# A transformer block on one core: the first products taken on the input with the channel scale alone, the token's scale and the shifts applied behind the sums

## The chip, the cores and the metric

The kernel runs on one core of a Trainium2 chip. The metric is the time of one execution in microseconds (us) on the device; for a kernel several runs are made and their median is given. A profile is the hardware profiler's record of one further execution.

## The reference, cut to what matters

The block is a feed-forward layer, a token mixer and a second feed-forward layer on 512 tokens of 1024 channels, in float32. The change touches the very first step only:

```
mod = silu(c) @ w_ada + b_ada            # 9 x 1024 numbers; m[0] a shift, m[1] a scale
h = rmsnorm(x, ffn1_pre_g) * (1 + m[1]) + m[0]
y = (silu(h @ w_gate) * (h @ w_up)) @ w_down
```

With r(token) = 1 / sqrt(mean over channels of x*x + eps), gamma(channel) = g * (1 + m[1]) and beta(channel) = m[0], this is h = x * r * gamma + beta. Since r belongs to the token and gamma and beta to the channel that a product sums over, h @ w = r * ((x * gamma) @ w) + beta @ w.

## The kernel before, in words

**Tiling.** Everything is held transposed: channels lie on the 128 partitions, in 8 blocks k, and the 512 tokens along them. A product of float32 quality is made of three float32r products: operand and weights are each split into a rounded high part and the rest (`hi`, `lo`), and hi·hi, lo·hi and hi·lo are summed in a bank of PSUM. `split` (L213) does this for a block of weights: ScalarE copies it rounded (L217), VectorE subtracts (L221). Raw weights arrive in a ring of 3 buffers, the split ones lie in rings of 6. `self.w2` hands out work tiles of 128x512 from a pool of 6.

**The opening** is `start` (L526). Three pairs of gate and up tiles (NSTART = 3, so six banks) are summed over the 8 channel blocks in step with the arrival of the modulation weights `wa` (8 MB, groups of 1, 1, 2, 2 and 2 blocks) and of the weights `w0` (one 384 KB block for each k). For each group `mod_rows` (L592) multiplies silu(c) into `wa` on TensorE, ScalarE copies the rows out, `mod_cols` (L604) turns them into columns of gamma and beta, and makes the `hi` and `lo` of those blocks of h: two ScalarE instructions (L618, L619) and one of VectorE (L620) for a block, on `u` = x * r, which `prepare` (L622) has made (L627) together with the split of w0[k]. Before any of that the whole input is squared and summed (L635 to L641), TensorE adds over the partitions (L645), root and reciprocal follow, and four transposes spread the result over a tile (L651, L653): r. `busy(n)` issues products that nobody reads. `first_product` (L694) is one of the 144 products of the opening. Then `act_tile` (L697) makes silu(gate) * up for the three pairs, and the gate and up products of the other 19 pairs follow (`product`, L322 to L325), each 24 matmuls over the 8 blocks of h in order, each in the next free bank.

**What sets the order.** TensorE and the DMA queue of SyncE (SP) execute in the order in which the program is written. ScalarE, VectorE and GpSimd get an order from a planner, which goes by the program's order and by the times it reckons. The DMAs of the opening are all issued by SP: cols, the four quarters of x, ident, then `wa` and `w0` in turn; from the fourth w0 on each has to wait for a raw buffer. Two background tasks start in this stage: `mod_task` (L473), the rest of the modulation, and `presplit` (L258), which splits weights of later stages through four buffers that lie where x lies, and fetches x again when it is done (L280). It can begin when x is no longer read.

Of the kernel before, what the change touches and what calls it, by code (L numbers as in the profile page):

```python
# [5 lines left out]
F32 = mybir.dt.float32  # L6
# [3 lines left out]
AF = mybir.ActivationFunctionType  # L10
# [4 lines left out]
P = 128  # L15
S = 512
D = 1024
ND = D // P
# [92 lines left out]
class Build:  # L111
# [414 lines left out]
    def start(self):  # L526
        nc = self.nc
        c = self.const
        self.cols = c.tile([P, NCOLS], F32, name="cols")
        nc.sync.dma_start(self.cols, self.i["cols"])  # L530
        self.X = self.big("X", XS)
        self.xd = self.dram.tile([P, ND, S], F32, name="xd")
        for q in range(4):
            nc.sync.dma_start(self.X.tiles[q // 2][:, 2 * (q % 2):2 * (q % 2) + 2], self.i["x"][:, 2 * q:2 * q + 2])
        self.ident = c.tile([P, P], F32, name="ident")
        nc.sync.dma_start(self.ident, self.i["ident"])
        w0 = [None] * ND

        groups = ((0,), (1,), (2, 3), (4, 5), (6, 7))
        wa = {}  # L540

        def fetch(g):
            if g < 2:
                t = self.blk("wa", AS[g], shape=(P, 8, 256))
                wa[g] = [t[:, :4], t[:, 4:]]
                nc.sync.dma_start(t, self.i["wa0"][g])
            else:
                wa[g] = [self.blk("wa", (AS[2:], YS, WS)[g - 2][e], shape=(P, 4, 512)) for e in range(2)]
                for e in range(2):
                    nc.sync.dma_start(wa[g][e], self.i["wa2"][g - 2, e])  # L550

        def fetch_w(k):
            w0[k] = Load(self.i["w0"][k], (6, P))
            w0[k].raw = self.ring.tile([P, 6, P], F32, name="raw", tag="raw", bufs=RAW)
            nc.sync.dma_start(w0[k].raw, w0[k].src)
            self.waiting += 1
        fetch(0)
        fetch_w(0)
        fetch(1)
        fetch_w(1)  # L560
        fetch(2)
        fetch_w(2)

        self.ones = c.tile([P, P], F32, name="ones")
        nc.gpsimd.memset(self.ones, 1.0)
        self.eps = c.tile([P, 1], F32, name="eps")
        nc.vector.memset(self.eps, EPS)

        self.sel = c.tile([P, 1], F32, name="sel")
# [12 lines left out]
        for pt in rows:  # L582
            nc.vector.memset(pt, 0.0)
        idle = self.bank("mm")

        def busy(n):

            for _ in range(n):
                nc.tensor.matmul(idle[:, :P], self.ones, self.ones, start=True, stop=True)
        accs, us = {}, {}  # L590

        def mod_rows(g):  # L592


            n = 256 * len(groups[g])
            acc = accs[g] = self.small.tile([P, 512], F32, name="macc", tag="macc", bufs=2)[:, :n]
            pt = rows[g % 2]
            for k in range(8):
                q = k % 4
                nc.tensor.matmul(pt[32 * q:32 * q + 1, :n], self.cs[:, k:k + 1], wa[g][k // 4][:, k % 4],  # L600
                                 start=(k < 4), stop=(k >= 4))
            nc.scalar.activation(acc, pt[:, :n], AF.Copy)

        def mod_cols(g):  # L604

            pt = rows[g % 2]
            k0, n = groups[g][0], len(groups[g])
            for q in range(2 * n):
                nc.tensor.matmul(pt[:, q:q + 1], accs[g][:, q * P:(q + 1) * P], self.sel, start=True, stop=True)
            mk = self.modc[:, :16].rearrange("p (j d) -> p d j", d=8)[:, k0:k0 + n]  # L610
            bk = self.col("b_ada", 0, 16).rearrange("p (j d) -> p d j", d=8)[:, k0:k0 + n]
            nc.vector.tensor_tensor(mk, pt[:, :2 * n].rearrange("p (d j) -> p d j", j=2), bk, op=ALU.add)
            gm = self.modc[:, 8 + k0:8 + k0 + n]
            nc.vector.scalar_tensor_tensor(gm, gm, 1.0, self.col("g1pre", k0, n), op0=ALU.add, op1=ALU.mult)
            for k in groups[g]:
                gamma, beta = self.modc[:, 8 + k:9 + k], self.modc[:, k:k + 1]
                h32 = self.last_h = self.w2("h32")
                nc.scalar.activation(hi[k], us[k], AF.Identity, scale=gamma, bias=beta)  # L618
                nc.scalar.activation(h32, us[k], AF.Identity, scale=gamma, bias=beta)  # L619
                nc.vector.tensor_tensor(lo[k], h32, hi[k].bitcast(F32), op=ALU.subtract)  # L620

        def prepare(g):  # L622

            for k in groups[g]:
                self.split(w0[k])
                us[k] = self.w2("u")
                nc.vector.tensor_tensor(us[k], self.X[k], r, op=ALU.mult)  # L627

        with self.tc.manual_schedule(engines={mybir.EngineType.PE}):
            busy(34)  # L630

            totals = []
            for k in range(ND):
                sq = self.w2("sq")
                nc.scalar.activation(sq, self.X[k], AF.Square)  # L635
                if k < 2:
                    totals.append(sq)
                else:
                    nc.vector.tensor_tensor(totals[k % 2], totals[k % 2], sq, op=ALU.add)
            total = totals[0]  # L640
            nc.vector.tensor_tensor(total, total, totals[1], op=ALU.add)  # L641
            pt = self.bank("wo")
            s, s2 = [self.small.tile([P, 4], F32, name="s", tag="s4") for _ in range(2)]
            for q in range(4):
                nc.tensor.matmul(pt[:, q:q + 1], total[:, q * P:(q + 1) * P], self.ones[:, 0:1], start=True, stop=True)  # L645
            nc.scalar.activation(s, pt[:, :4], AF.Sqrt, bias=self.eps, scale=1.0 / D)
            nc.vector.reciprocal(s2, s)
            pb = self.bank("wo")
            mod_rows(0)
            for q in range(4):  # L650
                nc.tensor.transpose(pb[:, q * P:(q + 1) * P], s2[:, q:q + 1].to_broadcast([P, P]), self.ident)  # L651
            r = self.w2("r")
            nc.scalar.activation(r, pb, AF.Copy)  # L653
            prepare(0)
            mod_cols(0)
            mod_rows(1)
            busy(4)
            prepare(1)
            banks = [self.bank("mm") for _ in range(4)] + [self.bank("wo") for _ in range(2)]
            for gi, g in enumerate(groups):  # L660
                for k in g:
                    if k + 3 < ND:
                        fetch_w(k + 3)
                    if k < 2:
                        fetch(k + 3)
                    if k == ND - 1:

                        for j in range(2 * NSTART):
                            for part in range(3):
                                self.first_product(banks[j], w0[k], j, k, part)  # L670
                    for part in range(3 if k < ND - 1 else 0):
                        for j in range(2 * NSTART):
                            self.first_product(banks[j], w0[k], j, k, part)

                        if part == 0 and k == g[-1] and gi + 1 < len(groups):
                            mod_cols(gi + 1)
                    self.alive -= 1

                    if k == g[0]:
                        nx = gi + 2 if gi == 0 else gi + 1  # L680
                        if gi != 1 and nx < len(groups):
                            mod_rows(nx)
                            prepare(nx)
                    if k >= 6:
                        self.feed(k - 5)

        nc.scalar.activation(warm, self.last_h[:, 0:1], AF.Silu)
        for f in range(NSTART):
            self.act_tile(f, banks[2 * f], banks[2 * f + 1], FULL)

    def first_product(self, ps, l, j, k, part):
        hi, lo = self.h
# [746 lines left out]
```

## Time and profile before

| what | value |
|---|---|
| runs: median (lowest to highest) | 1057.77 us (1055.55 to 1059.27) |
| the profiled execution's own time | 1056.43 us |
| its span, first to last instruction | 1054.7 us |
| TensorE busy | 1038.6 us, 98% of the span |
| VectorE busy, ScalarE busy | 625.8 us (59%), 478.3 us (45%) |
| mean granted TensorE clock | 0.996 |

The span lies within the execution's time; 1.73 us are around it. TensorE is nearly always busy, so a time is read off its row of instructions: what it has to do, and when it stands still. A timeline gives the start, the busy length and, in brackets, the idle time ahead of an instruction and who ended it.

### The profile page before, as it was taken

Reading aid. Unit: us, or ns where it says so; the run is one execution under the profiler, and the core shown is the slowest. Engines: PE = TensorE matmul, PEld = TensorE weight load, DVE = VectorE, ACT = ScalarE, POOL = GpSimd, SP = SyncE. Lnnn points to the kernel's source line nnn. Section 1 sums busy time; section 2 is a strip of 40 time slices with the busy share of each in tenths; the row PEclk is TensorE's granted clock in tenths of the full one; section 3 lists DMA queues with packets and bytes.
Section 4 is the critical chain, followed back from the end, with each engine's and each line's share of the span. In section 5 each row is a group of like instructions: output and inputs, shape, how many; then the busy total and the mean of one; then the engine's idle time right before and its main releaser. Section 6 shows DMA issues by size and latency. Waiting matters only on the chain.

```text
span 1054.7 us, 15248 instructions
## 1 busy us (share of the span) xinstructions
PE 1038.6 (98%) x5884; PEld 882.5 (84%) x5884; DVE 625.8 (59%) x1167; ACT 478.3 (45%) x782; POOL 88.4 (8%) x155
## 2 busy tenths in 40 slices
PE   8999999999999999999999999999999999999996
PEld 7788888888888999987776579999888888888896
DVE  5587877887774246579997843776322334333345
ACT  6564444343333457456776544645232222222252
POOL 0111111111110000000302610000000000000000
PEclk9999999999999999999999999999999999999998
DMA  9899899989997569593544431444333223333312
GB/s 366 320 378 360 336 354 328 335 308 357 333 342 281 214 222 349 179 355 120 204 161 144 152 117 41 162 141 135 125 120 100 93 79 109 100 99 100 100 41 80
DMA packets 57912, 217.32 MB, mean 206 GB/s; under 512 B 7128, under 2 KB 9496, under 8 KB 53232
## 3 DMA queue, kind: packets, MB, share of 16 engines
q1 hardware_dynamic: 43072, 164.86, 43.8%
q0 software_dynamic: 14768, 51.49, 13.5%
q8 instruction: 46, 0.75, 0.3%
q14 instruction: 26, 0.21, 0.1%
HBM read 193.24 MB, written 25.19 MB: 207 GB/s over the span
## 4 chain that ended last, share of the span: by engine, by line
PE 94%; DMA 3%; ACT 1%; issue 1%; DVE 1%; SPq 0%; DVEq 0%; ACTq 0%
PE mm L323 14%; PE mm L324 14%; PE mm L325 14%; PE wo L323 9%; PE wo L324 9%; PE wo L325 9%; PE mm L317 3%; PE mm L318 2%; PE mm L320 2%; PE mm L1251 2%; PE mm L694 1%; PE wo L317 1%; PE aux L1292 1%; PE wo L318 1%; PE wo L320 1%; DMA raw<-in_win_dram 1%
## 5 line engine op out<-in xcount | busy, mean ns | idle before, releaser
L217 ACT ACTIVATE hi<-raw 128x1024 fp32r<-128x1024 f32 (+2 forms) x192 | 197.2, 1031 | 377.6 <-PE mm L324 163.4
L221 DVE TENSOR_TENSOR lo<-raw,hi 128x1024 fp32r<-128x1024 f32 (+2 forms) x145 | 170.3, 1178 | 137.7 <-ACT hi L217 136.7
L323 PE MATMUL mm<-hhi,hi 128*128 128x512 f32 x368 | 144.1, 392 | 0.0
L325 PE MATMUL mm<-hhi,lo 128*128 128x512 f32 x368 | 143.3, 389 | 0.0
L324 PE MATMUL mm<-hlo,hi 128*128 128x512 f32 x368 | 143.2, 389 | 0.0
L323 PE MATMUL wo<-hhi,hi 128*128 128x512 f32 x280 | 111.1, 397 | 0.0
L323 PE MATMUL mm<-ahi,hi 128*128 128x256 f32 (+1 forms) x330 | 109.8, 334 | 0.0
L324 PE MATMUL mm<-alo,hi 128*128 128x256 f32 (+1 forms) x330 | 109.7, 333 | 0.0
L325 PE MATMUL mm<-ahi,lo 128*128 128x256 f32 (+1 forms) x330 | 109.7, 333 | 0.0
L325 PE MATMUL wo<-hhi,lo 128*128 128x512 f32 x280 | 109.6, 391 | 0.0
L324 PE MATMUL wo<-hlo,hi 128*128 128x512 f32 x280 | 109.0, 389 | 0.0
L325 PEld LDWEIGHTS mm<-hhi,lo 128*128 128x128 f32 x368 | 69.1, 188 | 14.5
L324 PEld LDWEIGHTS mm<-hlo,hi 128*128 128x128 f32 x368 | 69.1, 188 | 14.1
L323 PEld LDWEIGHTS mm<-hhi,hi 128*128 128x128 f32 x368 | 69.1, 188 | 14.1
L471 DVE SCALAR_TENSOR_TENSOR macc<-wa,cs,macc 128x512 f32<-128x512 f32 x98 | 73.2, 747 | 1.5
L324 PEld LDWEIGHTS mm<-alo,hi 128*128 128x128 f32 x330 | 62.7, 190 | 6.0
L325 PEld LDWEIGHTS mm<-ahi,lo 128*128 128x128 f32 x330 | 62.6, 190 | 6.0
L323 PEld LDWEIGHTS mm<-ahi,hi 128*128 128x128 f32 x330 | 62.5, 190 | 6.0
L324 PEld LDWEIGHTS wo<-hlo,hi 128*128 128x128 f32 x280 | 52.6, 188 | 12.0 <-issue 1.2
L323 PEld LDWEIGHTS wo<-hhi,hi 128*128 128x128 f32 x280 | 52.6, 188 | 11.9 <-issue 1.0
L325 PEld LDWEIGHTS wo<-hhi,lo 128*128 128x128 f32 x280 | 52.6, 188 | 11.1 <-issue 0.2
L317 PE MATMUL mm<-hhi,hi 128*128 128x256 f32 x232 | 59.1, 288 | 1.4 <-ACT hhi L382 1.4
(272 smaller groups left out, 1967.2 us busy)
## 6 DMA issues: line engine op xcount, KB each, us to landing
raw<-in_gu_dram SPq DMA_DIRECT2D x89, 512.0 KB, 4.4
wa<-in_wa_dram SPq DMA_DIRECT2D x36, 1024.0 KB, 10.0
lo<-pre SPq DMA_DIRECT2D x47, 512.0 KB, 5.2
pre<-pre POOLq DMA_DIRECT2D x36, 512.0 KB, 7.1
raw<-in_dn_dram SPq DMA_DIRECT2D x32, 448.0 KB, 4.0
raw<-in_win_dram SPq DMA_DIRECT2D x26, 512.0 KB, 6.2
raw<-in_dn_dram SPq DMA_DIRECT2D x22, 512.0 KB, 4.0
pre<-in_win_dram POOLq DMA_DIRECT2D x21, 512.0 KB, 6.5
```

The source lines that it names most:

```text
L217: nc.scalar.activation(l.hi, l.raw, AF.Copy)
L221: nc.vector.tensor_tensor(l.lo, l.raw, l.hi.bitcast(F32), op=ALU.subtract)
L317: self.nc.tensor.matmul(ps, l.hi[:, kt], xh[kt][:, tok], start=(q == 0), stop=False)
L318: self.nc.tensor.matmul(ps, l.lo[:, kt], xh[kt][:, tok], start=False, stop=False)
L320: self.nc.tensor.matmul(ps, l.hi[:, kt], xl[kt][:, tok], start=False, stop=(q == n - 1))
L323: self.nc.tensor.matmul(ps, l.hi[:, kt], xh[kt][:, tok], start=(first and q == 0), stop=False)
L324: self.nc.tensor.matmul(ps, l.hi[:, kt], xl[kt][:, tok], start=False, stop=False)
L325: self.nc.tensor.matmul(ps, l.lo[:, kt], xh[kt][:, tok], start=False, stop=(last and q == n - 1))
L471: nc.vector.scalar_tensor_tensor(acc, w[:, k], ck, acc, op0=ALU.mult, op1=ALU.add)
L694: self.nc.tensor.matmul(ps, w[:, j], x[k], start=(k == 0 and part == 0), stop=(k == ND - 1 and part == 2))
L1251: nc.tensor.matmul(ps[:, :n], self.q[rows, g, i * P:(i + 1) * P], self.k[rows, g, :n], start=True, stop=False)
L1292: nc.tensor.matmul(ps[64 * e:64 * e + 64, :P], self.v[:, t, 64 * h:64 * h + 64], pts[e][:, t * P:(t + 1) * P], start=(t == 0), stop=(t == i))
```

## The change: what it does

The first products are made on x * gamma in place of h. r comes in when a sum is read from PSUM, and beta @ w as a column added there (`first_act`). In detail:

- The order of the DMAs is now cols, `wa` 0, x 0, `w0` 0, `wa` 1, `w0` 1, `wa` 2 (two halves), x 1, `w0` 2, ident; the third and fourth quarter of x follow inside the loop.
- `busy(34)` becomes `busy(18)`, and a `busy(2)` is added. `mod_rows(1)` and its `prepare` move behind the first six products of k = 0; for k = 0 and 1 the next `mod_cols` stands behind the second part of the three.
- In `mod_cols` a block's `hi` is one ScalarE copy of x with gamma as the scale, `lo` one VectorE instruction. A third, new one per block adds w0[k] * beta into a tile `shifts`. The squares of x and their sums are made here, group by group.
- `scales` runs in three steps: the sum over partitions of two tiles (8 matmuls of one column, behind k = 4), the transposes, r and the load of the Silu table (inside k = 5), and the sum of `shifts` over the partitions (6 matmuls of one column, inside k = 7).
- The remaining 19 pairs still need the true h. `whole(k, r)` makes it in the same place: u = x * r, hi and the full value on ScalarE, lo on VectorE; blocks 0 to 5 behind k = 5, block 6 behind k = 6, block 7 behind the second `first_act`.

```diff
         fetch(0)
+        fetch_x(0)
         fetch_w(0)
         fetch(1)
         fetch_w(1)
         fetch(2)
+        fetch_x(1)
         fetch_w(2)
+        nc.sync.dma_start(self.ident, self.i["ident"])
...
             for k in groups[g]:
-                gamma, beta = self.modc[:, 8 + k:9 + k], self.modc[:, k:k + 1]
-                h32 = self.last_h = self.w2("h32")
-                nc.scalar.activation(hi[k], us[k], AF.Identity, scale=gamma, bias=beta)
-                nc.scalar.activation(h32, us[k], AF.Identity, scale=gamma, bias=beta)
-                nc.vector.tensor_tensor(lo[k], h32, hi[k].bitcast(F32), op=ALU.subtract)
+                gamma = self.modc[:, 8 + k:9 + k]
+                nc.scalar.activation(hi[k], self.X[k], AF.Copy, scale=gamma)
+                nc.vector.scalar_tensor_tensor(lo[k], self.X[k], gamma, hi[k].bitcast(F32), op0=ALU.mult, op1=ALU.subtract)
+            for k in groups[g]:
+                beta = self.modc[:, k:k + 1]
+                if k == 0:
+                    nc.vector.tensor_scalar(shifts, w0[k].raw, beta, None, op0=ALU.mult)
+                else:
+                    nc.vector.scalar_tensor_tensor(shifts, w0[k].raw, beta, shifts, op0=ALU.mult, op1=ALU.add)
+            for k in ((), (0, 1), (2, 3), (4, 5, 6, 7), ())[g]:
                 sq = self.w2("sq")
                 nc.scalar.activation(sq, self.X[k], AF.Square)
...
+        def whole(k, r):
+            u, h32 = self.w2("u"), self.w2("h32")
+            gamma, beta = self.modc[:, 8 + k:9 + k], self.modc[:, k:k + 1]
+            nc.vector.tensor_tensor(u, self.X[k], r, op=ALU.mult)
+            nc.scalar.activation(hi[k], u, AF.Identity, scale=gamma, bias=beta)
+            nc.scalar.activation(h32, u, AF.Identity, scale=gamma, bias=beta)
+            nc.vector.tensor_tensor(lo[k], h32, hi[k].bitcast(F32), op=ALU.subtract)
...
-            busy(34)
+            busy(18)
             mod_rows(0)
             prepare(0)
+            busy(2)
             mod_cols(0)
-            mod_rows(1)
             busy(4)
...
+                        if k < 2 and part == 0:
+                            mod_rows(gi + 1)
+                            prepare(gi + 1)
+                        if part == (1 if k < 2 else 0) and k == g[-1] and gi + 1 < len(groups):
                             mod_cols(gi + 1)
+                        if k == 5 and part == 1:
+                            r = next(late)
...
+                    if k == 4:
+                        next(late)
+                    for q in {5: range(6), 6: (6,)}.get(k, ()):
+                        whole(q, r)
...
         for f in range(NSTART):
-            self.act_tile(f, banks[2 * f], banks[2 * f + 1], FULL)
+            self.first_act(f, banks[2 * f], banks[2 * f + 1], r, bs)
+            if f == 1:
+                whole(ND - 1, r)
+    def first_act(self, f, pg, pu, r, bs):
+        sg, a, tg, tu = [self.w2(n) for n in ("sg", "a", "tg", "tu")]
+        nc.vector.tensor_tensor(tg, pg, r, op=ALU.mult)
+        nc.scalar.activation(sg, tg, AF.Silu, bias=bs[:, 2 * f:2 * f + 1])
+        nc.vector.tensor_tensor(tu, pu, r, op=ALU.mult)
+        nc.vector.scalar_tensor_tensor(a, tu, bs[:, 2 * f + 1:2 * f + 2], sg, op0=ALU.add, op1=ALU.mult)
+        nc.scalar.activation(self.act[0][f], a, AF.Copy)
+        nc.vector.tensor_tensor(self.act[1][f], a, self.act[0][f].bitcast(F32), op=ALU.subtract)
```

## Rows read from the trace of the kernel before

**Rows 1.** The page's first part: busy time, share of the span, instructions.

```profile
PE 1038.6 (98%) x5884; PEld 882.5 (84%) x5884; DVE 625.8 (59%) x1167; ACT 478.3 (45%) x782; POOL 88.4 (8%) x155
```

**Rows 2.** Chain of waits, 0 to 110 us: start, length, what.

```profile
4.80 10.95 DMA wa<-in_wa_dram
...
30.93 0.91 PE mm L694 x4
31.83 0.45 PE wo L694 x2
```

**Rows 3.** Timeline of TensorE, 1 to 20 us.

```profile
1.01 9.61 PE L589 MATMUL mm<-ones 128*128 128x128 f32 x68 [1.01 <-POOL sel L570]
12.27 1.05 PE L645 MATMUL wo<-ones,sq 128*128 128x1 f32 x8 [1.65 <-DVE sq L641]
13.25 1.04 PE L600 MATMUL aux<-wa,cs 128*1 128x256 f32 x16
14.23 0.65 PE L651 MATMUL wo<-ident,s 128*128 128x128 f32 x4
...
17.68 1.17 PE L694 MATMUL mm<-hhi,hi 128*128 128x512 f32 x4
```

**Rows 4.** Timeline of all engines and of TensorE, 44 to 62 us.

```profile
51.94 0.77 PEld L694 LDWEIGHTS mm<-hhi,hi 128*128 128x128 f32 x4 [0.47 <-ACT hhi L618]
...
60.28 0.39 PE L323 MATMUL mm<-hhi,hi 128*128 128x512 f32 x1
```

**Rows 5.** SP's timeline, and issue-to-landing (last column, us) of first x and third w0.

```profile
1.20 0.42 SPq L534 DMA_DIRECT2D X<-in_x_dram  x1
...
X<-in_x_dram SPq DMA_DIRECT2D x1, 512.0 KB, 4.4
...
9.47 0.33 SPq L555 DMA_DIRECT2D raw<-in_w_dram  x1
...
raw<-in_w_dram SPq DMA_DIRECT2D x1, 384.0 KB, 14.1
```

**Rows 6.** Timelines of ScalarE and VectorE, 19 to 67 us, and a page row.

```profile
19.75 0.16 DVE L612 TENSOR_TENSOR modc<-aux,cols 128x2 f32<-128x2 f32 x1
...
20.14 0.82 ACT L618 ACTIVATE hhi<-u,modc 128x512 fp32r<-128x512 f32 x1 [1.16 <-DVE modc L614]
...
51.09 0.80 ACT L618 ACTIVATE hhi<-u,modc 128x512 fp32r<-128x512 f32 x1
...
51.80 0.80 ACT L619 ACTIVATE h<-u,modc 128x512 f32<-128x512 f32 x1
...
54.98 1.28 ACT L687 ACT_TABLE_LOAD   x1
...
56.27 0.20 ACT L687 ACTIVATE warm<-h 128x1 f32<-128x1 f32 x1
...
58.28 1.06 ACT L701 ACTIVATE sg<-mm 128x512 f32<-128x512 f32 x2
...
59.73 1.28 DVE L702 TENSOR_TENSOR a<-mm,sg 128x512 f32<-128x512 f32 x2
...
62.59 2.00 ACT L217 ACTIVATE hi<-raw 128x1024 fp32r<-128x1024 f32 x2
...
64.14 2.35 DVE L221 TENSOR_TENSOR lo<-raw,hi 128x1024 fp32r<-128x1024 f32 x2
...
L471 DVE SCALAR_TENSOR_TENSOR macc<-wa,cs,macc 128x512 f32<-128x512 f32 x98 | 73.2, 747 | 1.5
```

**Rows 7.** Busy time by stretch (PE, PEld, DVE, ACT, POOL), granted clock, DMA share, GB/s.

```profile
10.00:20.00 10.00, 8.01 (x74) 5.81 (x73) 6.54 (x14) 5.18 (x10) 0.00 (x0) 1.00 1.02 418
...
60.00:80.00 20.00, 20.00 (x90) 16.54 (x89) 18.47 (x24) 12.14 (x16) 3.18 (x6) 1.00 0.97 382
```

**Rows 8.** Timeline of GpSimd: the first and the last fetch of the background split.

```profile
21.95 1.27 POOL L267 DMA_DIRECT2D pre<-in_dn_dram  x2 [20.43 <-ACT h L619]
...
320.07 1.05 POOL L281 DMA_DIRECT2D X<-in_x_dram  x2 [9.60 <-DMA pre<-pre]
```

More of the change, by code (lines that the diff above doesn't have):

```diff
@@ L532, in start @@
         self.xd = self.dram.tile([P, ND, S], F32, name="xd")
-        for q in range(4):
-            nc.sync.dma_start(self.X.tiles[q // 2][:, 2 * (q % 2):2 * (q % 2) + 2], self.i["x"][:, 2 * q:2 * q + 2])
         self.ident = c.tile([P, P], F32, name="ident")
-        nc.sync.dma_start(self.ident, self.i["ident"])
         w0 = [None] * ND
@@ L556, in fetch_w, with fetch_x @@
             self.waiting += 1
+        def fetch_x(q):
+            nc.sync.dma_start(self.X.tiles[q // 2][:, 2 * (q % 2):2 * (q % 2) + 2], self.i["x"][:, 2 * q:2 * q + 2])
         fetch(0)
+        fetch_x(0)
         fetch_w(0)
@@ L589, in busy @@
                 nc.tensor.matmul(idle[:, :P], self.ones, self.ones, start=True, stop=True)
-        accs, us = {}, {}
+        accs, totals = {}, []
+        shifts = c.tile([P, 6, P], F32, name="shifts")
         def mod_rows(g):
@@ L615, in mod_cols @@
             for k in groups[g]:
-                gamma, beta = self.modc[:, 8 + k:9 + k], self.modc[:, k:k + 1]
-                h32 = self.last_h = self.w2("h32")
-                nc.scalar.activation(hi[k], us[k], AF.Identity, scale=gamma, bias=beta)
-                nc.scalar.activation(h32, us[k], AF.Identity, scale=gamma, bias=beta)
-                nc.vector.tensor_tensor(lo[k], h32, hi[k].bitcast(F32), op=ALU.subtract)
-        def prepare(g):
-            for k in groups[g]:
[L625 to L629, printed above, removed]
-            busy(34)
-            totals = []
-            for k in range(ND):
+                gamma = self.modc[:, 8 + k:9 + k]
+                nc.scalar.activation(hi[k], self.X[k], AF.Copy, scale=gamma)
+                nc.vector.scalar_tensor_tensor(lo[k], self.X[k], gamma, hi[k].bitcast(F32), op0=ALU.mult, op1=ALU.subtract)
+            for k in groups[g]:
+                beta = self.modc[:, k:k + 1]
[4 more added lines that the diff above has]
+            for k in ((), (0, 1), (2, 3), (4, 5, 6, 7), ())[g]:
                 sq = self.w2("sq")
@@ L639, in start @@
                     nc.vector.tensor_tensor(totals[k % 2], totals[k % 2], sq, op=ALU.add)
-            total = totals[0]
-            nc.vector.tensor_tensor(total, total, totals[1], op=ALU.add)
-            pt = self.bank("wo")
+        def whole(k, r):
[5 more added lines that the diff above has]
+            nc.vector.tensor_tensor(lo[k], h32, hi[k].bitcast(F32), op=ALU.subtract)
@@ L643, in start, with prepare, scales @@
+        def prepare(g):
+            for k in groups[g]:
+                self.split(w0[k])
+        def scales():
+            pt = rows[1]
             s, s2 = [self.small.tile([P, 4], F32, name="s", tag="s4") for _ in range(2)]
-            for q in range(4):
-                nc.tensor.matmul(pt[:, q:q + 1], total[:, q * P:(q + 1) * P], self.ones[:, 0:1], start=True, stop=True)
+            for n, total in enumerate(totals):
+                for q in range(4):
+                    nc.tensor.matmul(pt[:, q:q + 1], total[:, q * P:(q + 1) * P], self.ones[:, 0:1],
+                                     start=(n == q == 0), stop=(n == 1), skip_group_check=True)
@@ L646, in start @@
             nc.scalar.activation(s, pt[:, :4], AF.Sqrt, bias=self.eps, scale=1.0 / D)
             nc.vector.reciprocal(s2, s)
-            pb = self.bank("wo")
+            yield
+            for q in range(4):
+                nc.tensor.transpose(pt[:, q * P:(q + 1) * P], s2[:, q:q + 1].to_broadcast([P, P]), self.ident)
+            r = self.w2("r")
+            nc.scalar.activation(r, pt, AF.Copy)
+            nc.scalar.activation(warm, r[:, 0:1], AF.Silu)
+            yield r
+            for j in range(2 * NSTART):
+                nc.tensor.matmul(pt[:, j:j + 1], shifts[:, j], self.ones[:, 0:1], start=True, stop=True)
@@ L649, in start @@
+            bs = c.tile([P, 2 * NSTART], F32, name="bs")
+            nc.vector.tensor_copy(bs, pt[:, :2 * NSTART])
+            yield bs
+        with self.tc.manual_schedule(engines={mybir.EngineType.PE}):
+            busy(18)
             mod_rows(0)
[L650 to L653, printed above, removed]
             prepare(0)
+            busy(2)
@@ L655, in start @@
             mod_cols(0)
-            mod_rows(1)
             busy(4)
-            prepare(1)
             banks = [self.bank("mm") for _ in range(4)] + [self.bank("wo") for _ in range(2)]
+            late = scales()
             for gi, g in enumerate(groups):
@@ L664, in start @@
                     if k < 2:
+                        fetch_x(k + 2)
                         fetch(k + 3)
@@ L670, in start @@
                                 self.first_product(banks[j], w0[k], j, k, part)
+                            if j == 0:
+                                bs = next(late)
                     for part in range(3 if k < ND - 1 else 0):
@@ L673, in start @@
                             self.first_product(banks[j], w0[k], j, k, part)
-                        if part == 0 and k == g[-1] and gi + 1 < len(groups):
+                        if k < 2 and part == 0:
+                            mod_rows(gi + 1)
+                            prepare(gi + 1)
+                        if part == (1 if k < 2 else 0) and k == g[-1] and gi + 1 < len(groups):
                             mod_cols(gi + 1)
+                        if k == 5 and part == 1:
+                            r = next(late)
                     self.alive -= 1
[L679 to L683, printed above, removed]
+                    if k == g[0] and k >= 2 and gi + 1 < len(groups):
+                        mod_rows(gi + 1)
+                        prepare(gi + 1)
+                    if k == 4:
+                        next(late)
+                    for q in {5: range(6), 6: (6,)}.get(k, ()):
+                        whole(q, r)
                     if k >= 6:
                         self.feed(k - 5)
-        nc.scalar.activation(warm, self.last_h[:, 0:1], AF.Silu)
         for f in range(NSTART):
-            self.act_tile(f, banks[2 * f], banks[2 * f + 1], FULL)
+            self.first_act(f, banks[2 * f], banks[2 * f + 1], r, bs)
+            if f == 1:
+                whole(ND - 1, r)
+    def first_act(self, f, pg, pu, r, bs):
+        nc = self.nc
+        sg, a, tg, tu = [self.w2(n) for n in ("sg", "a", "tg", "tu")]
[5 more added lines that the diff above has]
+        nc.vector.tensor_tensor(self.act[1][f], a, self.act[0][f].bitcast(F32), op=ALU.subtract)
     def first_product(self, ps, l, j, k, part):
```

## The prediction

> **What bounds the kernel now.** I read the page first: TensorE is busy for 98% of the span [rows 1]. What shortens the time must therefore give TensorE less to do or start it earlier, and what makes it stand still is paid in full. So I read its row in order. It opens with 9.6 us of products that nobody reads, idles 1.65 us for VectorE's sum of squares, and reaches the first useful product at 17.68 us [rows 3]. The chain of waits says what set that start: a DMA of `wa` that landed at 15.75 us [rows 2]. From 17.68 to 60.28, where the first gate product starts, it has one named wait, 0.47 us [rows 4]. Four products on `mm` banks and two on `wo` banks, the six of one part, follow each other in 0.91 + 0.45 = 1.36 us [rows 2]; 144 products are 24 such parts, 32.6 us. The other 10 us of the 42.6 are `mod_rows`, `mod_cols` and some 0.6 us of small gaps. The number to forecast is where 60.28 comes to lie, with later standstills added.
>
> **The earlier start.** Bytes on the DMA queue land in a steady sequence. The first quarter of x is issued at 1.20 and lands 4.4 us later, at 5.6, with 84 + 512 = 596 KB (cols, x) requested; the third `w0`, issued at 9.47, lands at 23.57, and with it 7444 KB have been asked for (cols 84, x 2048, ident 64, `wa` 4 x 1024, `w0` 3 x 384) [rows 5]. That is 17.97 us for 6848 KB, 2.62 us for 1000 KB. In the new order `wa` 0 is complete at 1108 KB, x 0 at 1620, `w0` 0 at 2004: an estimate of 6.9, 8.3 and 9.3 us. Then `mod_rows` 1.0 [rows 3], its copy, `mod_cols`, and on VectorE and ScalarE the column and the scaled copy: gamma at about 9.6. The split of `w0` 0 takes under 1.0 (two of 1024 columns take 2.00) and the scaled copy at most 0.8 (Identity with scale and bias) [rows 6]. One behind the other on ScalarE from 9.3 they end at 11.0. Start 11.0 in place of 17.68: **-6.7 us**. If the two overlap better, or bytes land 0.5 us sooner, it is 10.3; with `wa` late by 1 us, 12.
>
> **What TensorE has to do after the start.** All that lay in 42.6 stays. New behind the start are: `mod_rows(1)`, 1.0; the sums of squares, 16 instructions where 8 took 0.98 (12.27 to 13.25), so 2.0; the four transposes, 0.4 to 0.65; the sums of `shifts`, 12 instructions of the same kind, 1.5 [rows 3]. Together **+4.9 us**. The wait of 0.47, which came from ScalarE splitting weights ahead of `hi`, need not recur: **-0.5 us**. Without new waits the first gate product starts at 60.3 - 6.7 + 4.9 - 0.5 = 58.0, a gain of 2.3 us. That is small because most of the sums' work is only moved from ahead of the start to behind it.
>
> **What waits may come in the opening.** For k = 1 and 2 `mod_cols` now has one part, 1.36 us, to cover it, where it had two. From the first instruction on the column, at 19.75, to the start of `hi`, at 20.14, there are 0.4 us, and `hi` takes 0.8 at most [rows 6]: 1.2 us, just covered when both engines are free, and late by up to one split (1.0) when ScalarE is not. Two such places cost 0 to 2 us; I take 0.7. The DMAs keep ahead: `wa` of group 3 is complete at 9364 KB, at 28.6 us, and TensorE asks for it at 11.0 + 18.5 = 29.5 (9 parts of 1.36, `mod_rows` 1.0 and 1.83, the columns, 3.3 in sum). The background split cannot take bandwidth there, since x is still in use; before, it began at 21.95 [rows 8].
>
> **What VectorE and ScalarE must do before the first gate product can end.** This decides the sign. That product reads blocks 0 to 7 of the true h in order, three matmuls a block: block 7 is asked for 7/8 of 5.45 us after it starts, 58.0 + 4.8 = 62.8. r can be made only after the second part of k = 5; three parts of 1.36 for k = 7, three for k = 6, one for k = 5, the 1.5 of the shift sums and the transposes lie behind it, so it is there at about 58.0 - 11.0 + 0.7 = 47.5. In the 15.3 us between, by the lengths of [rows 6]:
> VectorE: `whole` has 16 instructions of 0.64 (two reads of PSUM took 1.28; the same form from SBUF is no dearer), 10.2. Ahead of them in the program stand `lo` and `shifts` of blocks 6 and 7, four instructions from 0.75 (512 columns, three operands) to 1.18 (1024 columns, 2.35 for two); I take 0.75 for `lo` and 1.0 for the 768 columns of `shifts`: 3.5, of which about 1.5 is done by 47.5, so 2.0 are left. Two splits of gate and up weights, 2.35. Ahead of `whole(7)` stand two `first_act`, four instructions of 0.64 to 0.75 each, 5.3. In sum 19.9 us for 15.3.
> ScalarE: the Silu table and its dummy, 1.4; 16 Identity at 0.71 (51.09 to 51.80), 11.4; two splits, 2.0; four of silu and copy at 0.53, 2.1: 16.9 us for 15.3.
> Served strictly in the program's order, block 7 is 4.6 us late. The planner may put what is needed later behind (one split, two of the last subtractions, one silu with its copy): 1.2 + 1.3 = 2.5 less on VectorE, 2.1 late. Nor is the bank of the first gate product free until VectorE has read it times r, an instruction that stands behind all of blocks 0 to 6. Between 2.1 and 4.6 I take **+2.7 us** for these waits, nearer the lower end: the planner does let ready work pass, but not always well, for the 0.47 us of [rows 4] came from a weight split that it had put ahead of a `hi` that TensorE needed. With the 0.7 of the opening: +3.4.
> The Silu table costs 1.28, and the next instruction starts 1.29 after it [rows 6]. [...]
>
> **After that.** In 60 to 80 us VectorE is busy for 18.47 of 20 [rows 7]; the backlog is worked off behind it, and splits run ahead of their use, so I cost it at nothing; without that cover, a split of 1.18 late for each of a few products, some 3 us. The background split starts when x 0 to 3 are read for the last time, at some 52 us in place of 21.95, and its last fetch, at 320 before, may slip by up to 30 us [rows 8]. x is needed again only behind the first layer's last products; I cost this at nothing too, and if that is late its price is the slip itself, at most those 30 us.
>
> **The sum**, against the profiled execution's own 1056.43: -6.7 + 4.9 - 0.5 + 0.7 + 2.7 = +1.1, 1057.5 us. The median of the runs is 1.34 above that execution: 1058.9, say **1059 us**. 0.3% is 3.2 us, about what a measurement of this kernel can tell from no change.
>
> **The rivals.** (a) *All covers hold*: the planner orders both engines by need, no new wait, start at 11.0 to 10.3. Time 1057.8 - 2.3 to - 3.2, 1055 us. For it: TensorE had one named wait in 42 us. Against: 19.9 us of work for 15.3. (b) *`whole` blocks the way* (slower): work tiles come from a pool of 6, r keeps one; a `first_act` needs four, a `whole` two. If they take turns, each `first_act` is a chain of about 0.64 + 0.53 + 0.75 + 0.53 + 0.64 = 3.1 us that starts behind block 6; ScalarE alone ends block 6 at 47.5 + 1.4 + 7 x 1.42 = 58.8, a weight split lies in between (1.0), then two chains 6.2, then block 7, 2.1: 68 in place of 62.8, 5.2 late, with the opening's 0.7 to 2: 1057.8 - 2.3 + 5.9 to + 7.2 = 1061.4 to 1062.7, and more if VectorE adds its own delay. It turns the sign to slower than can be told from no change when all new waits pass 2.3 + 3.2 = 5.5 us. For it: the pool's size; against: tiles are free as soon as read. (c) *The opening starves*: if `wa` of group 3 lands 2 us late, so does everything: 1060. [...]
>
> **How the numbers follow.** Forecast (waits of 1 to 5 us in all) 0.55; (a) 0.18; (b) 0.20; (c) 0.04; (d) 0.03. Faster by over 0.3% takes the better half of (a) and a little luck of the start: 0.12. Slower by over 0.3% takes (b), half of (c), (d) and the end of the forecast where waits pass 5 us: 0.31. The rest, 0.57, is within. The forecast's own range is 1056 to 1061; with (a) at one end and (b) at the other 1054.3 to 1065.
>
> **What would show it.** Right: the first L694-like product at 10.3 to 12 us; the first product of the pairs that follow at 58 to 60; two gaps of TensorE shortly before its seventh and eighth block, released by ScalarE or VectorE in `whole`; VectorE over 90% busy from 45 to 68 us. Wrong in the start: `wa` 0 not landed by 8 us. Wrong in the waits: no gap between 58 and 75 us (then (a)), or one of over 4 us (then (b)). Wrong in the cover: new gaps between 75 and 400 us, ended by a weight split or by a DMA.

## The result, and the profile after

The changed kernel takes 1067.87 us in the median (before, beside it on the same chip: 1057.16). The ratio is 1.0105 [1.009, 1.012], some 11 us slower. One of the four runs, at a mean granted clock of 0.75, took 1296.14 us: the median counts it, the ratio leaves it out, and the other three lie between 1066.81 and 1068.49. I had forecast 1059.0 with a range of 1054.3 to 1065.0: the sign of the sum was right, its size was not, and the time lies outside the range. The profiled execution took 1068.49 us with a span of 1066.7, against 1056.43 and 1054.7 before: between these two executions there are 12.06 us to find.

The page of the kernel after has nearly the same busy time of TensorE as [rows 1], and one group whose idle time is new (after the bar: busy, mean ns of one, then idle time just before and who ended it):

```profile
PE 1041.9 (98%) x5876; PEld 883.8 (83%) x5876; DVE 641.5 (60%) x1189; ACT 484.2 (45%) x790; POOL 88.4 (8%) x155
...
L323 PE MATMUL mm<-hhi,hi 128*128 128x512 f32 x368 | 144.8, 394 | 8.9 <-DVE tg L732 8.9
```

TensorE's waits, kernel after (total us, times, longest):

```profile
PE mm L323 <- DVE tg L732: 8.9, 1, 8.9
...
PE mm L742 <- ACT hhi L623: 1.5, 2, 1.0
```

So it is a single standstill. Its place, in the timeline of TensorE after, which answers to [rows 3, 4]:

```profile
9.80 1.14 PE L592 MATMUL mm<-ones 128*128 128x128 f32 x8
11.98 1.98 PE L742 MATMUL mm<-hhi,hi 128*128 128x512 f32 x4 [1.04 <-ACT hhi L623]
...
27.15 1.21 PE L742 MATMUL mm<-hhi,hi 128*128 128x512 f32 x4 [0.48 <-ACT hhi L623]
...
44.69 1.95 PE L660 MATMUL aux<-ones,sq 128*128 128x1 f32 x16
...
50.25 0.60 PE L666 MATMUL aux<-ident,s 128*128 128x128 f32 x4
...
56.62 0.39 PE L742 MATMUL mm<-hlo,hi 128*128 128x512 f32 x1
56.85 1.39 PE L673 MATMUL aux<-ones,shifts 128*128 128x1 f32 x12
58.10 0.48 PE L742 MATMUL mm<-hhi,hi 128*128 128x512 f32 x1
...
61.41 0.39 PE L742 MATMUL wo<-hlo,hi 128*128 128x512 f32 x1
70.69 0.77 PE L323 MATMUL mm<-hhi,hi 128*128 128x512 f32 x1 [8.90 <-DVE tg L732]
71.26 0.63 PE L324 MATMUL mm<-hlo,hi 128*128 128x512 f32 x1
...
73.70 0.39 PE L324 MATMUL mm<-hlo,hi 128*128 128x512 f32 x1
```

The opening's last product is over at 61.8 and the first gate product of the other pairs starts at 70.69 in place of 60.28. What it waits for is `tg`, VectorE's read of the first sum out of its `mm` bank: all six banks are full, and this read is the first to free one. Two rows of ScalarE (its copy that makes r, and its last read of block 6's u) and VectorE's timeline after:

```profile
50.94 0.60 ACT L668 ACTIVATE r<-aux 128x512 f32<-128x512 f32 x1 [0.24 <-PE aux L666]
...
64.59 0.49 DVE L469 TENSOR_SCALAR macc<-wa,cs 128x512 f32<-128x512 f32 x1 [1.03 <-DMA wa<-in_wa_dram]
...
68.30 0.80 ACT L645 ACTIVATE h<-u,modc 128x512 f32<-128x512 f32 x1
...
69.26 0.68 DVE L646 TENSOR_TENSOR hlo<-h,hhi 128x512 fp32r<-128x512 f32 x1
69.86 0.68 DVE L732 TENSOR_TENSOR tg<-mm,r 128x512 f32<-128x512 f32 x1
```

r has been there since 51.5 (ScalarE's copy starts at 50.94 and takes 0.60), and the bank's last product (56.62) ended at 57.0. Yet `tg` comes at 69.86, right behind the `lo` of block 5 (69.26), behind work that is needed far later (`macc`, 64.59) and an idle stretch of 1.03 us. So VectorE was not too slow for it: something else that `tg` needs was missing. The program gives `tg` a work tile from the pool of 6, r holds one of them, and `whole` takes two per block. That was the theory after the result: the pool hands the tile for `tg` over only when block 5 gives one back. The rivals: VectorE's and ScalarE's work for `whole` is itself too much (the prediction's term of 2.7, larger than thought), or TensorE lost its clock in the new gaps of the opening.

Busy time by stretch after (PE, PEld, DVE, ACT, POOL; granted clock, DMA share, GB/s):

```profile
10.00:20.00 10.00, 8.96 (x49) 6.04 (x49) 5.17 (x10) 3.22 (x6) 0.00 (x0) 0.83 1.01 410
...
60.00:70.00 10.00, 1.79 (x8) 1.13 (x6) 8.96 (x15) 8.03 (x11) 1.27 (x2) 0.84 0.99 403
70.00:80.00 10.00, 9.31 (x35) 7.65 (x36) 10.00 (x17) 4.53 (x7) 0.53 (x1) 0.82 0.21 78
80.00:400.00 320.00, 320.00 (x1592) 271.61 (x1591) 224.89 (x325) 137.91 (x174) 40.41 (x75) 1.00 0.87 322
```

The granted clock was not at full speed in three stretches: 0.83 in the opening, where [rows 7] has 1.00, and 0.84 and 0.82 around the standstill. From 80 to 400 us TensorE is busy for 320.00 of 320: nothing is lost there.

The account, from the rows: the start moved by -5.70 (17.68 to 11.98); from there to the end of the opening it takes 49.81 (61.79 - 11.98, with 61.79 = 70.69 - 8.90) in place of 42.60, +7.21; the wait +8.90. Sum +10.41, which is 70.69 - 60.28. Behind the wait the first seven products take 3.01 us to the start of the eighth (73.70) where seven at the later 0.227 (28 follow each other in 6.37 us from 73.70 to 80.07) take 1.59: +1.42. That makes 11.8 of the 12.0 by which the span grew. The granted clock was 0.50 from 70.69 to 73.39 and 1.00 from 73.70 to 80.

### The profile page after: what moved, and what is told of

Its sections match the earlier page's. It is cut to its first block, busy times and chain, and to the rows that moved or that the text cites. A ratio compares the mean times of both kernels' runs of the same rounds, so it can differ in the third digit from the quotient of the medians.

```text
span 1066.7 us, 15271 instructions
## 1 busy us (share of the span) xinstructions
PE 1041.9 (98%) x5876; PEld 883.8 (83%) x5876; DVE 641.5 (60%) x1189; ACT 484.2 (45%) x790; POOL 88.4 (8%) x155
## 4 chain that ended last, share of the span: by engine, by line
PE 92%; DMA 3%; ACT 2%; DVE 2%; issue 1%; SPq 0%; DVEq 0%; ACTq 0%
PE mm L323 14%; PE mm L324 13%; PE mm L325 13%; PE wo L323 9%; PE wo L324 9%; PE wo L325 9%; PE mm L317 3%; PE mm L318 2%; PE mm L320 2%; PE mm L1299 2%; DMA raw<-in_win_dram 2%; PE mm L742 2%; PE wo L317 1%; PE aux L1340 1%; PE wo L318 1%; PE wo L320 1%
## 5 line engine op out<-in xcount | busy, mean ns | idle before, releaser
L323 PE MATMUL mm<-hhi,hi 128*128 128x512 f32 x368 | 144.8, 394 | 8.9 <-DVE tg L732 8.9
L325 PE MATMUL mm<-hhi,lo 128*128 128x512 f32 x368 | 143.9, 391 | 0.0
L324 PE MATMUL mm<-hlo,hi 128*128 128x512 f32 x368 | 143.8, 391 | 0.0
L323 PE MATMUL wo<-hhi,hi 128*128 128x512 f32 x280 | 111.2, 397 | 0.0
L324 PE MATMUL mm<-alo,hi 128*128 128x256 f32 (+1 forms) x330 | 109.9, 333 | 0.0
L323 PE MATMUL mm<-ahi,hi 128*128 128x256 f32 (+1 forms) x330 | 109.8, 334 | 0.0
L325 PE MATMUL mm<-ahi,lo 128*128 128x256 f32 (+1 forms) x330 | 109.8, 333 | 0.0
L325 PE MATMUL wo<-hhi,lo 128*128 128x512 f32 x280 | 109.7, 392 | 0.0
L324 PE MATMUL wo<-hlo,hi 128*128 128x512 f32 x280 | 109.1, 390 | 0.0
L323 PEld LDWEIGHTS mm<-hhi,hi 128*128 128x128 f32 x368 | 69.5, 189 | 23.3 <-issue 9.3
L325 PEld LDWEIGHTS mm<-hhi,lo 128*128 128x128 f32 x368 | 69.4, 189 | 14.7
L324 PEld LDWEIGHTS mm<-hlo,hi 128*128 128x128 f32 x368 | 69.5, 189 | 14.0
L325 PEld LDWEIGHTS mm<-ahi,lo 128*128 128x128 f32 x330 | 62.7, 190 | 6.0
L324 PEld LDWEIGHTS mm<-alo,hi 128*128 128x128 f32 x330 | 62.8, 190 | 6.0
L323 PEld LDWEIGHTS mm<-ahi,hi 128*128 128x128 f32 x330 | 62.6, 190 | 6.0
L324 PEld LDWEIGHTS wo<-hlo,hi 128*128 128x128 f32 x280 | 52.6, 188 | 11.9 <-issue 1.2
L323 PEld LDWEIGHTS wo<-hhi,hi 128*128 128x128 f32 x280 | 52.6, 188 | 11.8 <-issue 1.0
L325 PEld LDWEIGHTS wo<-hhi,lo 128*128 128x128 f32 x280 | 52.6, 188 | 11.2 <-issue 0.2
```

The source lines that it names most:

```text
L323: self.nc.tensor.matmul(ps, l.hi[:, kt], xh[kt][:, tok], start=(first and q == 0), stop=False)
L324: self.nc.tensor.matmul(ps, l.hi[:, kt], xl[kt][:, tok], start=False, stop=False)
L325: self.nc.tensor.matmul(ps, l.lo[:, kt], xh[kt][:, tok], start=False, stop=(last and q == n - 1))
```

## The experiments

**One: tiles of their own for `whole`.** Eight tiles in memory that is free at that time replace the pool for u and the full value; nothing else changes.

```diff
+        ut, ht = self.temps("y0"), self.temps("y1")
+
         def whole(k, r):
-            u, h32 = self.w2("u"), self.w2("h32")
+            u, h32 = self.w2("u", ut), self.w2("h32", ht)
```

> The changed kernel with one edit: the work tiles of whole (u and the full value) come from two 4-tile buffers that lie idle in this stage, not from the pool of 6. The changed kernel stands still for 8.9 us ahead of the first gate product, until VectorE has read its bank times r (tg). Theory P (pool): that read waits for a work tile that a whole must give back. Then here it runs as soon as the sum is there, the first gate product starts at 62 to 63 us in place of 70.7, up to 3 us of waits for blocks of h remain, and the time falls by 5 to 8 us from 1067.9, to 1060-1063. Rival W (work): the blocks of h come no earlier, because VectorE and ScalarE are full; the wait only moves behind the first matmuls of that product, and the time stays at 1066-1068.

Measured: 1056.71 us (before, on the same chip: 1055.55), ratio 1.0011 [0.9996, 1.0026]; the loss is gone within what the interval can tell, more than expected. TensorE's timeline of this kernel:

```profile
12.16 1.19 PE L744 MATMUL mm<-hhi,hi 128*128 128x512 f32 x4 [1.04 <-ACT hhi L623]
...
60.09 0.39 PE L744 MATMUL wo<-hlo,hi 128*128 128x512 f32 x1
60.32 0.39 PE L323 MATMUL mm<-hhi,hi 128*128 128x512 f32 x1
...
62.36 0.61 PE L323 MATMUL mm<-hhi,hi 128*128 128x512 f32 x2
```

VectorE's:

```profile
56.99 0.68 DVE L734 TENSOR_TENSOR tg<-mm,r 128x512 f32<-128x512 f32 x1
...
70.00 0.68 DVE L648 TENSOR_TENSOR hlo<-temps,hhi 128x512 fp32r<-128x512 f32 x1
```

Its stretches:

```profile
10.00:20.00 10.00, 8.96 (x59) 6.06 (x62) 5.30 (x11) 3.46 (x7) 0.00 (x0) 1.00 1.01 408
...
60.00:70.00 10.00, 10.00 (x46) 8.29 (x45) 10.00 (x15) 10.00 (x15) 0.53 (x1) 1.00 1.02 417
70.00:80.00 10.00, 10.00 (x45) 8.29 (x45) 10.00 (x14) 6.52 (x8) 1.59 (x3) 1.00 0.60 205
```

`tg` is read at 56.99, 12.87 us earlier, and the gate product follows the opening without a wait. VectorE is now busy for 20.00 of 20 us from 60 to 80 and the `lo` of block 7 ends only at 70.7, 10 us after the first gate product began, and still TensorE is busy throughout. It works on more than one product at a time there: one product alone goes L323, L324, L325 in turn, and at 62.36 two L323 follow each other. So the volume of work on VectorE and a late block 7 cost nothing. The gap of 1.04 us ahead of the first product is here too, with a clock of 1.00 behind it.

**Two: the other user of the pool gets its own tiles.** `whole` stays in the pool.

```diff
+        self.ft = self.temps("y1")
...
-        sg, a, tg, tu = [self.w2(n) for n in ("sg", "a", "tg", "tu")]
+        sg, a, tg, tu = [self.w2(n, self.ft) for n in ("sg", "a", "tg", "tu")]
```

> The changed kernel with one edit: the four work tiles of first_act come from an idle 4-tile buffer; whole keeps the pool of 6. P: the read of the first bank runs at about 59 us, the gate product starts at 62; block 5 of h, which came at 70 us, is now waited for inside that product, so less comes back than with the tiles for whole: 3 to 6 us, 1062-1065. W: under 2 us, 1066-1068.

Measured: 1057.91, ratio 1.0014 [1.0001, 1.0028], better than the 1062 to 1065 expected. VectorE and then TensorE of this kernel:

```profile
58.06 0.68 DVE L734 TENSOR_TENSOR temps<-mm,r 128x512 f32<-128x512 f32 x1
...
71.79 0.68 DVE L645 TENSOR_TENSOR u<-X,r 128x512 f32<-128x512 f32 x1
```

```profile
60.21 0.39 PE L744 MATMUL wo<-hlo,hi 128*128 128x512 f32 x1
60.43 0.39 PE L323 MATMUL mm<-hhi,hi 128*128 128x512 f32 x1
```

Either user of the pool may leave it, and the wait is gone. Here block 7 isn't even begun (its u, the row at 71.79) 11 us after the gate product started, and TensorE doesn't wait for it.

**Three: the gaps of the opening filled.** More products that nobody reads keep TensorE busy up to the first useful one.

```diff
-            busy(18)
+            busy(22)
             mod_rows(0)
             prepare(0)
-            busy(2)
+            busy(3)
             mod_cols(0)
-            busy(4)
+            busy(7)
```

> The changed kernel with one edit: more idle products in TensorE's gaps ahead of the first product (22, 3 and 7 in place of 18, 2 and 4), nothing else. In the changed kernel the granted clock is 0.83 on the mean of 10 to 20 us, and the first six products take 2.76 us where six take 1.36. Theory C: the gaps ahead of 12 us brought the clock down; with them filled the first part takes about 1.4 us, r and all behind it come 1.6 us sooner, and the time is 1066.3. Rival: the level falls in this stretch whatever TensorE did, and nothing changes, 1067.9; or the filling delays the columns, 1068-1069.

Measured: 1067.38, ratio 1.0108 [1.0084, 1.0131], as slow as the change itself. Stretches, then the wait of TensorE and two rows of its timeline:

```profile
10.00:20.00 10.00, 10.00 (x72) 7.66 (x68) 4.87 (x10) 3.47 (x6) 0.00 (x0) 1.00 1.01 409
...
60.00:70.00 10.00, 0.93 (x5) 0.43 (x3) 8.75 (x14) 7.23 (x11) 0.98 (x2) 0.75 1.01 413
70.00:80.00 10.00, 9.97 (x33) 8.05 (x34) 10.00 (x17) 5.17 (x8) 0.53 (x1) 0.73 0.17 48
```

```profile
PE mm L323 <- DVE tg L732: 9.1, 1, 9.1
...
70.03 0.77 PE L323 MATMUL mm<-hhi,hi 128*128 128x512 f32 x1 [9.11 <-DVE tg L732]
...
75.29 0.41 PE L323 MATMUL mm<-hhi,hi 128*128 128x512 f32 x1
```

The clock stayed at 1.00 in the opening and the products ended earlier, at 60.9 in place of 61.8, but `tg` was late all the same. The first gate product came at 70.03, 0.66 us earlier; behind the wait twelve products were slow (70.03 to 75.29, 5.26 us where twelve at 0.227 take 2.72, +2.54) in place of seven (+1.42), which took that back. As a test of the gaps it is inconclusive: experiments one, two, four and five keep the gap of 1.04 us, and their clock from 10 to 20 us is 1.00 too.

**Four: the true h not made.** This kernel leaves out `whole`; the later products run on x * gamma. It measures what the remaining work of the change costs.

```diff
-                    for q in {5: range(6), 6: (6,)}.get(k, ()):
-                        whole(q, r)
...
-            if f == 1:
-                whole(ND - 1, r)
```

> The changed kernel without whole: the true h is never made, and the later gate and up products run on x times gamma (that part of the computation is left out). P and W agree that the wait of 8.9 us and the low clock behind it go: first gate product at 61.7 to 62.5 us, 1057-1059. It gives the price of making h in that place, and what start and added work on TensorE are worth by themselves: if it comes out within 2 us of the kernel before (1057.2), the earlier start is eaten up by the added work alone.

Measured: 1057.31, ratio 1.0008 [0.9994, 1.0022]; its row of TensorE:

```profile
60.38 0.39 PE L323 MATMUL mm<-hhi,hi 128*128 128x512 f32 x1
```

Against experiment one, 1.0011, this is no difference: once tiles are there, making h costs nothing that can be measured. And without it the change still gains nothing, since what the earlier start brings is spent on the work added behind it.

**Five: one tile more in the pool.** Only r moves out of it, so that five tiles for `whole` and `first_act` become six.

```diff
-            r = self.w2("r")
+            r = self.w2("r", self.temps("y1"))
```

> The changed kernel with one edit: r lies in an idle buffer, so the pool of 6 work tiles has one more for whole and first_act. Theory P (the read of the first bank waits for a work tile): the read moves ahead by one block of whole, 2 to 3 us; the wait of 8.9 us ahead of the first gate product becomes 6 to 7, and the ratio to the kernel before falls from 1.0105 to about 1.008. If only tiles for first_act itself mattered, or if the two runs with eight and four more tiles won by something else, nothing moves: 1.0105.

Measured: 1066.52, ratio 1.0091 [1.0077, 1.0105]. ScalarE's copy that makes r (here the tile `temps`), VectorE and then TensorE of this kernel:

```profile
48.94 0.60 ACT L668 ACTIVATE temps<-aux 128x512 f32<-128x512 f32 x1 [0.18 <-PE aux L666]
...
64.97 0.68 DVE L646 TENSOR_TENSOR hlo<-h,hhi 128x512 fp32r<-128x512 f32 x1
65.57 1.22 DVE L221 TENSOR_TENSOR lo<-raw,hi 128x1024 fp32r<-128x1024 f32 x1
66.70 0.68 DVE L732 TENSOR_TENSOR tg<-mm,temps 128x512 f32<-128x512 f32 x1
...
67.96 1.29 DVE L646 TENSOR_TENSOR hlo<-h,hhi 128x512 fp32r<-128x512 f32 x2
```

```profile
67.53 0.77 PE L323 MATMUL mm<-hhi,hi 128*128 128x512 f32 x1 [7.68 <-DVE tg L732]
...
71.94 0.48 PE L324 MATMUL mm<-hlo,hi 128*128 128x512 f32 x1
```

With one tile more `tg` stands behind block 4 and ahead of block 5 (the row at 67.96 holds the `lo` of blocks 5 and 6). It comes at 66.70 in place of 69.86, but not all of these 3.16 us are the tile's: in this execution the opening started at 11.62 and ran at full clock (1.00 from 10 to 20 us), so that r was made 2.00 us earlier (48.94 in place of 50.94). From r to `tg` it is 17.76 us in place of 18.92. The tile is worth 1.2 us, which is also what the wait fell by (8.90 to 7.68), less than the 2 to 3 us expected. In the time this can't be told from the change itself, since the intervals of 1.0091 and 1.0105 overlap; what the experiment shows is the order. Of the 3.16 us by which the gate product came sooner, some 0.7 went to the clock: the slow products behind the wait are ten here (67.53 to 71.94, 4.41 us where ten at 0.227 take 2.27, +2.14; granted clock 0.59 from 60 to 70 us, 0.89 from 70 to 80) against +1.42.

**Six: the old order of the DMAs in experiment one.** All of x and ident come first again, as before the change.

```diff
+        for q in range(4):
+            nc.sync.dma_start(self.X.tiles[q // 2][:, 2 * (q % 2):2 * (q % 2) + 2], self.i["x"][:, 2 * q:2 * q + 2])
+        nc.sync.dma_start(self.ident, self.i["ident"])
...
-        fetch_x(0)
...
-            busy(18)
+            busy(38)
...
-                        fetch_x(k + 2)
```

> The kernel with whole's tiles from idle buffers (1056.71 us, ratio 1.0011) with one part of the change undone: all of x and ident are fetched ahead of wa and w0, as before, and the idle products are lengthened to cover it. Theory S (the start sets the end, one for one): wa 0 lands at 12.3 us in place of 7, the first product starts at 16 to 17 in place of 12.2, the sum of squares is no longer late, and the first gate product comes at 64 to 65: ratio 1.005 to 1.006, about 1061. Rival: something later than the start decides (a DMA, r, the blocks of h), and the time stays within 1.5 us of 1056.7.

Measured: 1060.86, ratio 1.0037 [1.0023, 1.0051], where experiment one had 1.0011. Its row of TensorE:

```profile
16.25 1.19 PE L743 MATMUL mm<-hhi,hi 128*128 128x512 f32 x4 [0.26 <-ACT hhi L623]
...
63.38 0.39 PE L323 MATMUL mm<-hhi,hi 128*128 128x512 f32 x1
```

A start 4.09 us later gives a gate product 3.06 us later: the start is worth some three quarters of itself in this place, and not one for one as expected.

**Seven: a version that beats both.** Experiment one with three edits more, run together and not told apart: the squares are issued behind the scaled copy, the low part of the first weights behind gamma, and the two sums of squares are added on VectorE, which halves their products on TensorE.

```diff
+            if g == 0:
+                with self.tc.issue_after(made.ins):
+                    nc.vector.tensor_tensor(w0[0].lo, w0[0].raw, w0[0].hi.bitcast(F32), op=ALU.subtract)
...
-                nc.scalar.activation(sq, self.X[k], AF.Square)
+                with self.tc.issue_after(copied.ins):
+                    nc.scalar.activation(sq, self.X[k], AF.Square)
...
-            for n, total in enumerate(totals):
-                for q in range(4):
-                    nc.tensor.matmul(pt[:, q:q + 1], total[:, q * P:(q + 1) * P], self.ones[:, 0:1],
-                                     start=(n == q == 0), stop=(n == 1), skip_group_check=True)
+            nc.vector.tensor_tensor(totals[0], totals[0], totals[1], op=ALU.add)
+            for q in range(4):
+                nc.tensor.matmul(pt[:, q:q + 1], totals[0][:, q * P:(q + 1) * P], self.ones[:, 0:1], start=True, stop=True)
```

(`made` is the instruction that makes gamma, `copied` the scaled copy, and `split` leaves out the low part for k = 0.)

> The kernel with whole's tiles from idle buffers, with three more edits that leave the result as it is: the squares are issued only behind the scaled copy of their group and the low part of w0 0 behind gamma (in the changed kernel two squares stood ahead of the copy of the rows, and that split ahead of gamma), and the two tiles of squares are added on VectorE, so that 4 one-column matmuls are left where there were 8. Theory S: first product at 10.8 in place of 12.2 (-1.4), TensorE 0.9 less to do, the first gate product at 58 in place of 60.3: ratio 0.998 to 0.9995, some 1 us faster than the kernel before. Rival: what is won at the start is lost again in a wait for wa or for the sum of squares: ratio 1.001 as without these edits.

Measured: 1054.20 against 1057.07 for the kernel before on the same chip, ratio 0.9973 [0.9963, 0.9984]: faster by 0.27%, a small gain, but clear of its interval. Its rows of TensorE:

```profile
11.14 1.21 PE L746 MATMUL mm<-hhi,hi 128*128 128x512 f32 x4 [0.27 <-ACT hhi L626]
...
58.26 0.39 PE L323 MATMUL mm<-hhi,hi 128*128 128x512 f32 x1
```

The first product is 1.02 us earlier than in experiment one, the first gate product 2.06.

## Why the prediction was wrong, step by step

**The start: 11.0 forecast, 11.98 found.** The mechanism held, and the value lies inside the bracket of 10.3 to 12; in the other kernels with this order it was 11.62 to 12.65. Two instructions that I had not put there stood in the way: ScalarE squared two blocks of x ahead of the copy of the rows, and VectorE subtracted the first weights' low part ahead of gamma. A row of ScalarE and the timeline of VectorE after:

```profile
7.79 1.15 ACT L633 ACTIVATE sq<-X 128x512 f32<-128x512 f32 x2 [3.18 <-DMA X<-in_x_dram]
...
10.14 0.96 DVE L221 TENSOR_TENSOR lo<-raw,hi 128x768 fp32r<-128x768 f32 x1
11.02 0.15 DVE L619 SCALAR_TENSOR_TENSOR modc<-modc,cols 128x1 f32<-128x1 f32 x1
```

The copy of the rows follows the squares at 8.85, though the products that it copies (7.25, 1.04 us) were over by 8.3. Where both are moved behind, in experiment seven, the start is 11.14.

**The added work: +4.9 forecast.** From row to following row the sums take 1.81 (44.69 to 46.50), the transposes 0.35, the sums of `shifts` 1.25; with `mod_rows(1)` at 1.0 that is 4.4. The whole stretch from the first product to the gate product is the better check: in experiment one, at full clock, 60.32 - 12.16 = 48.16, where 42.6 + 4.9 - 0.5 + 0.7 = 47.7 was forecast: 5.6 more than before. Of these, 4.4 are the terms above; the other 1.2 lie in the 144 products themselves, which take 35.5 us from row to row there and 34.3 before, where the prediction reckoned 32.6; for this it had no term but the 0.7. The wait of 0.5 us that I let go came back at another place (0.48 at 27.15), and is part of the 0.7. This term and the start together make the change worth nothing (experiment four: 1.0008), where a gain of 2.3 - 0.7 = 1.6 us was forecast.

**The waits before the gate products: this step failed.** I forecast +2.7, argued from 19.9 us of VectorE's work in 15.3 us and a block 7 asked for at 62.8. That VectorE's product with r is no dearer from SBUF than from PSUM held: 0.68 us each (71.79 and 58.06 in experiment two). The runs show 8.9 us in its place, at the first gate product and not at its last block, and of another cause: the read that frees the first bank had no work tile. Two premises fell. First, TensorE does not take the blocks of one product in order without a break there: the planner orders TensorE's work too once the opening's hand-written order ends, and runs ready products on other banks meanwhile, as experiments one and two show with a block 7 that is late by 5.6 us and by some 10 (asked for some 4.8 us after the gate product's start) and no wait. What the section on the kernel before says of TensorE's order holds for the opening only. Second, I said that the bank of the first gate product is not free until `tg` has been read behind blocks 0 to 6, but priced that read as if it came as soon as VectorE had time. It has to have a tile first. The sign that the prediction itself gave for this case, one gap of over 4 us between 58 and 75, is what came. Two sums of the prediction are off by 0.2 us and decide nothing: 58.0 - 11.0 + 0.7 is 47.7, not 47.5, and a start at 10.3 makes rival (a) -3.0, not -3.2.

**Rival (b)** named the pool, and gave it 0.20 and 1061.4 to 1062.7 "and more". The mechanism was right, its place and size were not: I let `first_act` and `whole` take turns ahead of block 7, where the tile is short ahead of the very first read, with all six banks still full. The tie to the tiles is shown from both sides (experiments one and two), and by a dose (experiment five: one tile, one block, 1.2 us). Why the planner gives `tg` its tile behind block 5 and not earlier is not shown, since the profile shows no tile being handed over. A count fits it, which no run tests: in the program u and the full value of block 6, and then `sg` and `a`, ask for a tile ahead of `tg`. Given out in that order as tiles come back, the tile for `tg` comes at 69.10 here (ScalarE's last read of block 6's u, 68.30 + 0.80) and at 65.65 in experiment five (the `lo` of block 4, 64.97 + 0.68), each just ahead of the read at 69.86 and 66.70.

**Rival (c)**, an opening that starves, did not come: no wait of TensorE for `wa` is in its list of waits after.

**Rival (d), the clock**, got 0.03 and came true in part. In the opening of the kernel after, the first four products take 1.98 us, where experiment one has 1.19, the mean granted clock from 10 to 20 us is 0.83, and the opening takes 49.81 us where the same opening takes 48.16 in experiment one and 48.23 in five (59.85 - 11.62), both at 1.00: 1.6 us. The gap ahead is the same 1.04 us in all of them, so the gap alone doesn't decide it; what else does stays open. It may belong to this execution alone: the other two that the ratio counts took 1066.81 and 1067.24 us, 1.7 and 1.3 less than the profiled one, but they have no profile. I had not thought of the other place: the standstill of 8.9 us itself, after which seven products take 0.43 us each instead of 0.227, with a granted clock of 0.50 over the first six (70.69 to 73.39). That is +1.42 on top of the wait. The slow products are seven here, ten in experiment five and twelve in experiment three; these are three kernels with one profile each, so whether the number changes from one execution of a kernel to the next is not shown.

**After that: nothing forecast, nothing found.** 320.00 us of 320 are busy from 80 on. The background split began at 60.58 (forecast: some 52), and its last fetch of x was issued at 336.16 in place of 320.07, within the 30 us allowed.

**Together:** -5.7 + 5.6 for start and work at full clock, + 1.6 and + 1.4 for the clock, + 8.9 for the tile: +11.8. Without the last three there is no change, which is what experiment one measured.

## What to carry to other kernels

When a change adds users to a pool of work tiles, follow the pool as one follows an engine: list who holds a tile when the first read of a full PSUM bank is due, because a read that has no tile for its result keeps the bank, and TensorE behind it, even where VectorE has idle time (here 8.90 us of TensorE, with 1.03 us of idle VectorE in them). In a timeline the mark of it is a reader that comes late right behind another user of the same pool, with its inputs long there and less urgent work or idle time ahead of it. And a start that comes earlier is worth only what is not moved behind it: here 5.5 us of start bought 5.6 us of work.

## What the runs showed of the hardware

A standstill of TensorE cost more than its length: behind idle times of 8.90, 7.68 and 9.11 us the next seven, ten and twelve products went at some 0.43 us each in place of 0.227, a loss of 1.4, 2.1 and 2.5 us. In the kernel after the granted clock was 0.50 where they were slow (70.69 to 73.39) and 1.00 behind it (73.70 to 80). Gaps of 1.04 us ahead of the first product were followed by a granted clock of 1.00 from 10 to 20 us in four kernels (experiments one, two, four and five) and of 0.83 in one (the kernel after). The load of the Silu table took 1.28 us and came after r here, and as in [rows 6] the next instruction started 1.29 us after it (51.56 to 52.85).
